# The SSD state product as three fp32r passes in a one-core hybrid decoder step

## The chip, the cores and the metric

One core of one Trainium2 chip runs the whole program. The metric is device time in microseconds (us) of one execution; the kernel before has a median of 1965.07 us over three runs (1964.24 to 1966.66). Less is better.

## What is computed

One inference step of a decoder layer: a norm, one combined input projection, three parallel groups (a gated linear recurrence, dilated-window attention, a Mamba-2 state-space group called SSD), and one output projection. The prompt has 2048 tokens, and 8 samples bring 4 tokens each. The change touches the SSD group of the prompt, which works through 16 chunks of 128 tokens and carries a state from chunk to chunk:

```python
xdt = x * dt[..., None]
scores = jnp.einsum('bcihn,bcjhn->bcijh', Ch, Bh) * decay
y_diag = jnp.einsum('bcijh,bcjhp->bcihp', scores, xdt)
to_end = jnp.exp(cum[:, :, -1:, :] - cum)
chunk_states = jnp.einsum('bcjhn,bcjh,bcjhp->bchpn', Bh, to_end, xdt)
...
h_last, h_starts = lax.scan(step, h0, ...)     # h = chunk_decay * h + chunk_states
y_off = jnp.einsum('bcihn,bchpn->bcihp', Ch, h_starts) * jnp.exp(cum)[..., None]
```

`chunk_states` is the product that the change rewrites: B transposed, times x·dt·to_end, for each chunk.

## The kernel before, in words

The program runs in stages: norm and input projections, the samples, attention, and from about 1440 us on the last stage, in which the output projection of chunk c and the SSD of the chunks ahead of it run interleaved.

Large products are made in three fp32r passes by `mm3` (lines 81 to 84): each operand is split into a high part in fp32r and a low part (the rest), and high·high, high·low and low·high are summed in PSUM. The output projection `out_chunk` (line 1434) does this for each chunk: 2 halves of the model width times 16 weight tiles times 3 passes of 128x512, 96 matmuls (tile `ops`). After each of the 32 steps it may let the SSD generator `ssd_part` (line 1270) take one step, 15 SSD steps to 32 projection steps. A framework schedules each engine's instructions in one fixed order and sets the waits; each engine runs its order without overtaking.

The SSD of a chunk has two head groups, g = 0 and 1. For each:

- `ssd_open` (line 694, once a chunk): `gp`, the products of C and B; `gm`, their mask, on DVE; `tpb`, B transposed on PE, copied by ACT to the one tile `bt` (line 710).
- `ssd_decay` (line 719): ACT takes exp(cum) from the freshly loaded `sg` into `ecB`; DVE subtracts in eight pieces (line 728), ACT takes the exponential (line 730), DVE multiplies by `gm` (line 731).
- `ssd_x` (line 734): PE transposes x (`tpx`), DVE multiplies by dt to `xdt` (line 744), POOL multiplies that by `tend` into the tile `xte` (line 750), and x by D (line 1292).
- `yd` (line 1298, from `sg` and `xdt`) and `yo` (line 1303, from the state `hT`) on PE.
- DVE forms y in four steps (lines 1311 to 1314): `yo` times `ecB`, plus `yd`, plus `xb`, times the gate `zt`. `yd` and `yo` are in PSUM, all else in SBUF.
- `group_norm` (line 754): ACT squares, POOL adds twice (lines 758, 759), PE sums over partitions (`rs`), ACT makes the reciprocal norm `rB`, DVE multiplies (line 766).
- the state product `stp` (line 1322), one fp32 matmul of 128x512 that PE carries out as two instructions; POOL decays `hT` (line 1327) and DVE adds `stp` (line 1328).
- the split of y for the output projection: ACT `sh` (line 1335), DVE `sl` (line 1336).

Chunk 0 runs on slab tiles (`ssd_early`, line 1248) while attention ends, and only it forms `xte` late (line 1320). The tile `sg` has one buffer: the load for the next half is issued when `yd` has read the last one. Weight tiles of the output projection (`wo`) are still being loaded and split on ACT and DVE (lines 1009, 1010) while chunks 0 and 1 run.

```python
xte = ck.tile([128, 8, 64], F32, tag="xte", name="xte", bufs=1)
pool.tensor_tensor(out=xte[:n], in0=xdt[:n], in1=tend[...], op=OP.mult)
...
pe.matmul(stp, lhsT=bt[:, g], rhs=xte.rearrange("p h d -> p (h d)"), start=True, stop=True)
```

Of the kernel before, what the change touches and what calls it, by code (L numbers as in the profile page):

```python
# [32 lines left out]
def tile_hybrid_step(ctx: ExitStack, tc: tile.TileContext, A):  # L33
# [1214 lines left out]
    def ssd_early():  # L1248
# [9 lines left out]
        ck0.own = {"gm": [piece(c_[0], 512, 2)], "bt": [piece(c_[0], 768, 2)], "xdt": [piece(c_[2], 512, 8, 64), piece(c_[3], 0, 8, 64)]}  # L1258
        for g in range(2):
# [10 lines left out]
    def ssd_part(c):  # L1270
# [5 lines left out]
        for g in range(2 if c == 0 else 0):  # L1276
            sg = ssd_decay(c, g, ck, gm)
            yield
            xb, xdt, _ = ssd_x(c, g, ck, ps6, False)
            pool.tensor_tensor(out=xb, in0=xb, in1=dF[:, 4 * g:4 * g + 4, None].to_broadcast([128, 4, 128]), op=OP.mult)  # L1280
            ahead[g] = sg, xb, xdt
            yield
        for g in range(2):
# [38 lines left out]
            pe.matmul(stp, lhsT=bt[:, g], rhs=xte.rearrange("p h d -> p (h d)"), start=True, stop=True)  # L1322
            if c == 0:
# [326 lines left out]
```

## Time and profile before

| what | value |
|---|---|
| median of 3 runs | 1965.07 us (1964.24 to 1966.66) |
| the profiled execution | 1966.87 us, of which its span is 1965.1 us |
| PE busy | 1906.4 us, 97% of the span |
| DVE, ACT, POOL busy | 1065.2 us (54%), 780.9 us (40%), 271.9 us (14%) |
| granted TensorE clock over the span | 0.992 of full speed |
| state product `stp` | 32 products, 64 matmul instructions |

The span is the time between the first and last recorded instruction; the rest of the 1966.87 us lies around it. A busy PE is not a PE at its peak: matmuls overlap, so a duration of one is longer than the distance from its start to the next start, and that distance is what a pass costs. Names stand as output<-inputs; buffer numbers are left out. The number in brackets behind a timeline row is the idle time of that engine just before it, and what ended it.

### The profile page before, as it was taken

To read this page: it belongs to the slowest core of one execution; us is meant where nothing else is said; L and a number is where in the kernel's file an instruction comes from. 1 tells how busy PE (TensorE), PEld (TensorE's weight loads), DVE (VectorE), ACT (ScalarE), POOL (GpSimd) and SP (SyncE) were. 2 spreads that over 40 slices of the span, in tenths; PEclk is the share of its full clock that TensorE was granted. 3 is DMA by queue.
4 is the path that set the end of the run, shared out by engine and by line. 5 is a ranking of instruction groups with operands and counts; after the bars stand their busy time and mean duration, and the time that the engine had idled before them with its cause. 6 is when DMAs were issued, how large, how long until landed. Compare 5 with 4: busy or idle time off the path is not lost.

```text
span 1965.1 us, 35826 instructions
## 1 busy us (share of the span) xinstructions
PE 1906.4 (97%) x14178; PEld 1559.9 (79%) x14178; DVE 1065.2 (54%) x2338; ACT 780.9 (40%) x1530; POOL 271.9 (14%) x346
## 2 busy tenths in 40 slices
PE   7999999999999999999999899999998999999998
PEld 7998888888888888887866686777776878677876
DVE  7414444444423666664322215666777777667774
ACT  6412637272712222223133315666564333324332
POOL 0100111111110111111000100000012232322231
PEclk9999999999999999998999999999999999999999
DMA  7422121121223222225477651442375444434441
GB/s 234 127 83 67 46 65 54 55 76 55 76 83 95 72 78 67 72 68 148 139 199 201 185 185 52 145 137 77 116 216 156 140 128 128 124 110 131 124 140 65
DMA packets 278388, 222.03 MB, mean 113 GB/s; under 512 B 34738, under 2 KB 234402, under 8 KB 278220
## 3 DMA queue, kind: packets, MB, share of 16 engines
q1 hardware_dynamic: 278220, 219.73, 37.3%
q8 instruction: 112, 1.84, 0.4%
q14 instruction: 56, 0.46, 0.1%
HBM read 150.81 MB, written 68.86 MB: 112 GB/s over the span
## 4 chain that ended last, share of the span: by engine, by line
PE 85%; DMA 4%; ACT 4%; DVE 3%; issue 1%; SPq 1%; POOL 1%; DVEq 0%; ACTq 0%; POOLq 0%
PE mm L82 15%; PE mm L84 15%; PE mm L83 15%; PE ops L84 5%; PE ops L83 5%; PE ops L82 5%; PE pt L1179 3%; ACT sr L1151 2%; PE o L1215 2%; PE s L1124 2%; PE yd L1298 2%; PE yo L1303 1%; PE s L1103 1%; DMA x<-in_x_prompt_dram 1%; PE mmt L82 1%
## 5 line engine op out<-in xcount | busy, mean ns | idle before, releaser
L82 PE MATMUL mm<-xh,wh 128*128 128x512 f32 (+2 forms) x1600 | 563.3, 352 | 1.6 <-DVE h L846 0.9
L83 PE MATMUL mm<-xl,wh 128*128 128x512 f32 (+2 forms) x1600 | 561.7, 351 | 0.0
L84 PE MATMUL mm<-xh,wl 128*128 128x512 f32 (+2 forms) x1600 | 561.0, 351 | 0.0
L82 PEld LDWEIGHTS mm<-xh,wh 128*128 128x128 f32 x1600 | 301.7, 189 | 44.0 <-issue 4.3
L84 PEld LDWEIGHTS mm<-xh,wl 128*128 128x128 f32 x1600 | 300.9, 188 | 41.0 <-issue 2.9
L83 PEld LDWEIGHTS mm<-xl,wh 128*128 128x128 f32 x1600 | 301.4, 188 | 39.0 <-issue 1.7
L146 POOL TENSOR_TENSOR wr<-wr,gC 128x1024 f32<-128x1024 f32 x40 | 79.1, 1978 | 415.7 <-DMA wr<-in_w_in_dram 370.8
L443 DVE SCALAR_TENSOR_TENSOR o<-u,ssdc,o 128x512 f32<-128x512 f32 (+1 forms) x216 | 128.8, 617 | 5.1
L1151 ACT ACTIVATE sr<-sr,nm 128x384 f32<-128x384 f32 (+3 forms) x128 | 97.9, 771 | 23.3 <-DVE nm L1147 14.1
L650 ACT ACTIVATE o<-o 128x512 f32<-128x512 f32 (+2 forms) x60 | 33.1, 552 | 149.4 <-DVE o L443 77.3
L148 DVE SCALAR_TENSOR_TENSOR wl<-wr,wh 128x1024 fp32r<-128x1024 f32 x40 | 48.9, 1223 | 68.4 <-ACT wh L147 68.4
L1062 ACT COPY ptsb<-pt 128x512 f32<-128x512 f32 x96 | 52.5, 583 | 75.0 <-PE pt L1179 74.9
L728 DVE TENSOR_SCALAR sg<-sg,cum 128x128 f32<-128x128 f32 (+1 forms) x256 | 72.9, 344 | 16.5 <-ACT ecB L726 16.5
L82 PE MATMUL mmt<-wh,xh 128*128 128x256 f32 (+3 forms) x272 | 78.5, 291 | 1.6 <-ACT xh L254 0.8
L83 PE MATMUL mmt<-wl,xh 128*128 128x256 f32 (+3 forms) x272 | 77.8, 287 | 0.3
L1179 PE MATMUL pt<-ident,sr 128*128 128x128 f32 x576 | 75.2, 281 | 2.8 <-ACT sr L1151 1.8
L84 PE MATMUL mmt<-wh,xl 128*128 128x256 f32 (+3 forms) x272 | 77.9, 288 | 0.0
L1112 DVE CUSTOM_DVE_ANT_1 sr<-s,bias 128x256 f32<-128x256 f32 x128 | 46.5, 419 | 56.9 <-PE s L1124 29.7
L441 DVE TENSOR_SCALAR o<-u,ssdc 128x512 f32<-128x512 f32 (+1 forms) x72 | 40.5, 575 | 65.8 <-ACT u L423 57.6
L1179 PEld LDWEIGHTS pt<-ident,sr 128*128 128x128 f32 x576 | 63.6, 143 | 15.1 <-issue 8.8
L423 ACT COPY u<-mm 128x512 f32<-128x512 f32 (+1 forms) x80 | 39.6, 495 | 88.6 <-PE mm L84 79.6
L726 ACT ACTIVATE ecB<-sg 64x512 f32<-64x512 f32 x60 | 37.8, 630 | 91.7 <-DMA sg<-d_cum 77.1
(526 smaller groups left out, 3585.0 us busy)
## 6 DMA issues: line engine op xcount, KB each, us to landing
wr<-in_w_in_dram SPq DMA_DIRECT2D x40, 512.0 KB
sg<-d_cum SPq DMA_DIRECT2D x30, 512.0 KB
d_xbc<-o SPq DMA_DIRECT2D x36, 256.0 KB
x<-in_x_prompt_dram SPq DMA_DIRECT2D x32, 256.0 KB
kc<-in_cache_attn_k_dram SPq DMA_DIRECT2D x32, 256.0 KB
vt<-in_cache_attn_v_dram SPq DMA_DIRECT2D x32, 256.0 KB
xres<-in_x_prompt_dram SPq DMA_DIRECT2D x32, 256.0 KB
out_dram<-ot SPq DMA_DIRECT2D x32, 256.0 KB
```

Source lines behind the costliest of these rows:

```text
L82: pe.matmul(out, lhsT=wh, rhs=xh, start=start, stop=False)
L83: pe.matmul(out, lhsT=wh, rhs=xl, start=False, stop=False)
L84: pe.matmul(out, lhsT=wl, rhs=xh, start=False, stop=stop)
L146: pool.tensor_tensor(out=wr, in0=wr, in1=gC[:, :, None].to_broadcast([128, 8, 128]), op=OP.mult)
L148: dve.scalar_tensor_tensor(out=wl, in0=wr, scalar=scale, in1=wh.bitcast(F32), op0=OP.mult, op1=OP.subtract)
L441: dve.tensor_scalar(out=o, in0=v(0), scalar1=w[:, 0:1], scalar2=b, op0=OP.mult, op1=OP.add)
L443: dve.scalar_tensor_tensor(out=o, in0=v(t), scalar=w[:, t:t + 1], in1=o, op0=OP.mult, op1=OP.add)
L728: dve.tensor_scalar(out=sg[:n, h], in0=sg[:n, h], scalar1=cum[:n, c, 8 * g + h:8 * g + h + 1], scalar2=0.0, op0=OP.subtract, op1=OP.min)
L1062: act.copy(out=out, in_=in_)
L1112: dve.tensor_tensor_reduce(out=sr[e][r][:, nk:].rearrange("p (w c) -> p w c", w=2), in0=pw[e][:, j].rearrange("p (w c) -> p w c", w=2), in ...
L1151: act.activation(out=sr[e][r], in_=sr[e][r], func=AF.Exp, bias=nm[:, e, r:r + 1], accum_out=ll[:, e, r:r + 1])
L1179: pe.transpose(tp[:, r], sr[e][r][:, 128 * g:128 * g + 128], ident)
```

## The change

The state product becomes three fp32r passes through `mm3`. For that, `bt` becomes a pair of tiles (ACT casts the high part, DVE subtracts for the low part), and `xte` becomes a pair: POOL multiplies `xdt` by `tend` in place, ACT casts it to the high part, POOL subtracts for the low part. Since `xdt` is overwritten, the product with `tend` moves from `ssd_x` to behind the forming of y, for every chunk, and `xdt` gets two buffers. `ecB` goes: exp(cum) is written into the tile `y`, which is allocated earlier. `rB` gets one buffer, and four small constant tiles move to a pool that closes before the last stage. Lines of the kernel after stand up to four higher than before.

```diff
-        bt = ck.tile([128, 2, 128], F32, tag="bt", name="bt", bufs=1)
+        bt = [ck.tile([128, 2, 128], F32R, tag=f"bt{i}", name="bt", bufs=1) for i in "hl"]
...
-        act.copy(out=bt, in_=tp[:, 0:2])
+        act.copy(out=bt[0], in_=tp[:, 0:2])
+        dve.tensor_tensor(out=bt[1], in0=tp[:, 0:2], in1=bt[0].bitcast(F32), op=OP.subtract)
...
-        xdt = ck.tile([128, 8, 64], F32, tag="xdt", name="xdt", bufs=1)
+        xdt = ck.tile([128, 8, 64], F32, tag="xdt", name="xdt", bufs=2)
...
     def to_end(c, g, ck, xdt):
-        n = TT[c][1]
-        xte = ck.tile([128, 8, 64], F32, tag="xte", name="xte", bufs=1)
-        pool.tensor_tensor(out=xte[:n], in0=xdt[:n], in1=tend[:n, c, 8 * g:8 * g + 8, None].to_broadcast([n, 8, 64]),
-                           op=OP.mult)
-        return xte
+        xh_, xl_ = [ck.tile([128, 512], F32R, tag=f"xte{i}", name="xte", bufs=1) for i in "hl"]
+        xte = xdt.rearrange("p h d -> p (h d)")
+        pool.tensor_tensor(out=xdt, in0=xdt, in1=tend[:, c, 8 * g:8 * g + 8, None].to_broadcast([128, 8, 64]), op=OP.mult)
+        act.copy(out=xh_, in_=xte)
+        pool.tensor_tensor(out=xl_, in0=xte, in1=xh_.bitcast(F32), op=OP.subtract)
+        return xh_, xl_
...
-                ecB = ck.tile([128, 4, 128], F32, tag="ecB", name="ecB", bufs=1)
-                sg = ssd_decay(c, g, ck, gm, ecB)
+                y = ck.tile([128, 4, 128], F32, tag="yt", name="y")
+                sg = ssd_decay(c, g, ck, gm, y)
                 yield
-                xb, xdt, xte = ssd_x(c, g, ck, ps6)
+                xb, xdt = ssd_x(c, g, ck, ps6)
...
-                dve.tensor_tensor(out=y, in0=yo, in1=ecB, op=OP.mult)
+                dve.tensor_tensor(out=y, in0=y, in1=yo, op=OP.mult)
...
             yield
+            xte = to_end(c, g, ck, xdt)
             norm = group_norm(ck, ps6, y, 128, dve if c == 0 else pool)
             next(norm)
             yield
-            if c == 0:
-                xte = to_end(c, g, ck, xdt)
             stp = psA.tile([128, 512], F32, tag="mm", name="stp")
-            pe.matmul(stp, lhsT=bt[:, g], rhs=xte.rearrange("p h d -> p (h d)"), start=True, stop=True)
+            mm3(stp, bt[0][:, g], bt[1][:, g], *xte, True, True)
```

How the orders of two engines change, at a place that repeats from chunk 3 to chunk 15. On POOL, one half of a chunk, before: the product with D, the product with `tend`, the decay of the state, the two sums of squares.

```order
L1292 TENSOR_TENSOR xb<-xb,dF 128x512
L750 TENSOR_TENSOR xte<-xdt,tend 128x512
L1327 TENSOR_TENSOR hT<-hT,dec 128x512
L758 TENSOR_TENSOR sq<-sq 128x256
L759 TENSOR_TENSOR sq<-sq 128x128
```

The same half after the change:

```order
L1297 TENSOR_TENSOR xb<-xb,dF 128x512
L752 TENSOR_TENSOR xdt<-xdt,tend 128x512
L1331 TENSOR_TENSOR hT<-hT,dec 128x512
L754 TENSOR_TENSOR xte<-xdt,xte 128x512
L761 TENSOR_TENSOR sq<-sq 128x256
L762 TENSOR_TENSOR sq<-sq 128x128
```

The product with `tend` is now the in-place one, in the same place of the order; the low part of `xte` stands behind the decay of the state, and ahead of the sums.

On ACT, from the reciprocal norm of a chunk's second half to the split of the next chunk's rows, before:

```order
L764 ACTIVATE rB<-rs,eps_t 128x128
L765 ACTIVATE rB<-rB 128x128
L1335 CAST sh<-y 128x512
L710 COPY bt<-tpb 128x256
L730 ACTIVATE sg<-sg 128x1024
L1443 CAST mh<-ym 128x512
```

and after:

```order
L767 ACTIVATE rB<-rs,eps_t 128x128
L768 ACTIVATE rB<-rB 128x128
L710 CAST bt<-tpb 128x256
L1339 CAST sh<-y 128x512
L731 ACTIVATE sg<-sg 128x1024
L753 CAST xte<-xdt 128x512
L1447 CAST mh<-ym 128x512
```

The transposed B is now cast ahead of `sh` and not behind it, and the high part of `xte` stands behind the exponential. On DVE one row comes in per chunk, the low part of `bt`, between `gm` and the last piece of the subtraction. On PE the two instructions of `stp` become three, in the same places from chunk 3 on; in chunks 0 to 2 the order of PE, DVE and ACT is mixed anew.

## Rows read from the trace of the kernel before

**Rows 1.** The page: busy time per engine; shares of the chain that ended last.
```profile
PE 1906.4 (97%) x14178; PEld 1559.9 (79%) x14178; DVE 1065.2 (54%) x2338; ACT 780.9 (40%) x1530; POOL 271.9 (14%) x346
...
PE 85%; DMA 4%; ACT 4%; DVE 3%; issue 1%; SPq 1%; POOL 1%; DVEq 0%; ACTq 0%; POOLq 0%
```

**Rows 2.** Busy time by stretch: us, PE, PEld, DVE, ACT, POOL busy (x), clock, DMA, GB/s.
```profile
1440.00:1500.00 60.00, 54.07 (x333) 38.86 (x331) 52.31 (x87) 33.23 (x57) 16.72 (x15) 1.00 0.66 193
1500.00:1940.00 440.00, 435.73 (x2444) 339.20 (x2445) 307.44 (x592) 160.11 (x334) 128.12 (x144) 1.00 0.41 124
```

**Rows 3.** PE timeline around one state product: start, us, engine, line, operation, [idle].
```profile
1633.53 0.39 PE L83 MATMUL ops<-wo11l,sh 128*128 128x512 f32 x1
1633.76 0.39 PE L84 MATMUL ops<-wo11h,sl 128*128 128x512 f32 x1
1633.98 1.02 PE L1322 MATMUL stp<-xte,bt 128*128 128x512 f32 x2
1635.08 0.40 PE L83 MATMUL ops<-wo12l,sh 128*128 128x512 f32 x1
```

**Rows 4.** The chain that ended last, around the same product: start, us, what.
```profile
1634.14 0.86 PE stp L1322 x2
```

**Rows 5.** DVE timeline of the second half of a chunk.
```profile
1629.38 0.69 DVE L1311 TENSOR_TENSOR y<-yo,ecB 128x512 f32<-128x512 f32 x1 [2.61 <-PE yo L1303]
1630.10 0.69 DVE L1312 TENSOR_TENSOR y<-y,yd 128x512 f32<-128x512 f32 x1
1630.89 0.69 DVE L1313 TENSOR_TENSOR y<-y,xb 128x512 f32<-128x512 f32 x1
1631.62 0.69 DVE L1314 TENSOR_TENSOR y<-y,zt 128x512 f32<-128x512 f32 x1
1640.08 0.68 DVE L744 TENSOR_TENSOR xdt<-tpx,dtT 128x512 f32<-128x512 f32 x1
```

**Rows 6.** PEld timeline: first weight load of yd in four halves.
```profile
1536.17 0.85 PEld L1298 LDWEIGHTS yd<-sg,xdt 128*64 128x64 f32 x16 [0.36 <-DVE xdt L744]
...
1641.11 0.85 PEld L1298 LDWEIGHTS yd<-sg,xdt 128*64 128x64 f32 x16 [0.35 <-DVE xdt L744]
...
1765.14 0.85 PEld L1298 LDWEIGHTS yd<-sg,xdt 128*64 128x64 f32 x16 [0.43 <-DVE xdt L744]
...
1915.19 0.85 PEld L1298 LDWEIGHTS yd<-sg,xdt 128*64 128x64 f32 x16 [0.36 <-DVE xdt L744]
```

**Rows 7.** POOL timeline of the same half as rows 5.
```profile
1627.03 1.04 POOL L750 TENSOR_TENSOR xte<-xdt,tend 128x512 f32<-128x512 f32 x1
1629.42 1.05 POOL L1327 TENSOR_TENSOR hT<-hT,dec 128x512 f32<-128x512 f32 x1 [1.35 <-PE yo L1303]
```

**Rows 8.** DVE, then POOL, at the first chunk: operations of both at once.
```profile
1452.74 1.03 DVE L1314 TENSOR_TENSOR y<-y,c 128x512 f32<-128x512 f32 x1
...
1452.17 1.05 POOL L750 TENSOR_TENSOR xte<-c,tend 128x512 f32<-128x512 f32 x1 [3.17 <-DVE wo7l L1010]
```

**Rows 9.** DVE timeline, end of a first half (to 1765), and two further xdt.
```profile
1535.24 0.68 DVE L744 TENSOR_TENSOR xdt<-tpx,dtT 128x512 f32<-128x512 f32 x1
...
1761.26 0.41 DVE L703 TENSOR_TENSOR gm<-gp,tri 128x256 f32<-128x256 f32 x1
1761.59 0.27 DVE L728 TENSOR_SCALAR sg<-sg,cum 128x128 f32<-128x128 f32 x1
1764.41 0.68 DVE L744 TENSOR_TENSOR xdt<-tpx,dtT 128x512 f32<-128x512 f32 x1
...
1914.33 0.68 DVE L744 TENSOR_TENSOR xdt<-tpx,dtT 128x512 f32<-128x512 f32 x1
```

**Rows 10.** ACT timeline of the same first half.
```profile
1761.38 0.62 ACT L1335 CAST sh<-y 128x512 fp32r<-128x512 f32 x1 [2.14 <-DVE y L766]
1761.90 0.37 ACT L710 COPY bt<-tpb 128x256 f32<-128x256 f32 x1
1762.16 1.06 ACT L730 ACTIVATE sg<-sg 128x1024 f32<-128x1024 f32 x1
```

More of the change, by code (lines that the diff above doesn't have):

```diff
@@ L64, in tile_hybrid_step @@
     aB = const.tile([128, 16], F32, name="aB")
-    srep = const.tile([128, 2, 16], F32, name="srep")
+    srep = mid.tile([128, 2, 16], F32, name="srep")
     dec = const.tile([128, 17, 16], F32, name="dec")
@@ L70, in tile_hybrid_step @@
     pool.memset(ones, 1.0)
-    decs = const.tile([128, 8, NB], F32, name="decs")
-    bsel = const.tile([96, NB], F32, name="bsel")
+    decs = mid.tile([128, 8, NB], F32, name="decs")
+    bsel = mid.tile([96, NB], F32, name="bsel")
     qs = mid.tile([128, 4, NS], F32, name="qs")
@@ L77, in tile_hybrid_step @@
     fold = const.tile([128, NS], F32, name="fold")
-    sp8 = const.tile([128, 2, 4], F32, name="sp8")
+    sp8 = mid.tile([128, 2, 4], F32, name="sp8")
     ngc = const.tile([128, 8], F32, name="ngc")
@@ L732, in ssd_decay, with ssd_x @@
         return sg
-    def ssd_x(c, g, ck, ps, ends=True):
+    def ssd_x(c, g, ck, ps):
         t0, n = TT[c]
@@ L742, in ssd_x @@
         xv = tp[:n].rearrange("p j (e d) -> p (j e) d", e=2)
-        xdt = ck.tile([128, 8, 64], F32, tag="xdt", name="xdt", bufs=1)
+        xdt = ck.tile([128, 8, 64], F32, tag="xdt", name="xdt", bufs=2)
         dve.tensor_tensor(out=xdt[:n], in0=xv, in1=dtT[:n, c, hs, None].to_broadcast([n, 8, 64]), op=OP.mult)
-        return xb, xdt, to_end(c, g, ck, xdt) if ends else None
+        return xb, xdt
     def to_end(c, g, ck, xdt):
-        n = TT[c][1]
-        xte = ck.tile([128, 8, 64], F32, tag="xte", name="xte", bufs=1)
-        pool.tensor_tensor(out=xte[:n], in0=xdt[:n], in1=tend[:n, c, 8 * g:8 * g + 8, None].to_broadcast([n, 8, 64]),
-                           op=OP.mult)
-        return xte
+        xh_, xl_ = [ck.tile([128, 512], F32R, tag=f"xte{i}", name="xte", bufs=1) for i in "hl"]
[4 more added lines that the diff above has]
+        return xh_, xl_
     def group_norm(ck, ps, y, n, add=pool):
@@ L762, in group_norm @@
         pe.matmul(rs[:, :n], lhsT=ones, rhs=sq[:, 0], start=True, stop=True)
-        rB = ck.tile([128, n], F32, tag="rB", name="rB")
+        rB = ck.tile([128, n], F32, tag="rB", name="rB", bufs=1)
         act.activation(out=rB, in_=rs[:, :n], func=AF.Ln, scale=1.0 / 512, bias=eps_t)
@@ L1251, in piece @@
             return t[:, o:o + m * n].rearrange("p (m t) -> p m t", m=m)
-        c_ = [big(f"c0{i}", XC, F32) for i in range(8)]
-        bc, tri0 = piece(c_[0], 0, 4), c_[7][:, 512:640]
+        c_ = [big(f"c0{i}", XC, F32R if i == 3 else F32) for i in range(8)]
+        bt = piece(c_[3], 512, 4)
+        bc, tri0 = piece(c_[0], 0, 4), c_[0][:, 768:896]
         sp.dma_start(out=bc, in_=d_xbc[1024:, 0:128].rearrange("(m p) t -> p m t", p=128))
@@ L1257, in ssd_early @@
         early[(0, "bc")], late["tri0"] = bc, tri0
-        ck0.own = {"gm": [piece(c_[0], 512, 2)], "bt": [piece(c_[0], 768, 2)], "xdt": [piece(c_[2], 512, 8, 64), piece(c_[3], 0, 8, 64)]}
+        ck0.own = {"gm": [piece(c_[0], 512, 2)], "bth": [bt[:, 0:2]], "btl": [bt[:, 2:4]], "xdt": [piece(c_[2], 512, 8, 64), piece(c_[7], 512, 8, 64)]}
         for g in range(2):
@@ L1278, in ssd_part @@
             yield
-            xb, xdt, _ = ssd_x(c, g, ck, ps6, False)
+            xb, xdt = ssd_x(c, g, ck, ps6)
             pool.tensor_tensor(out=xb, in0=xb, in1=dF[:, 4 * g:4 * g + 4, None].to_broadcast([128, 4, 128]), op=OP.mult)
@@ L1287, in ssd_part @@
             else:
-                ecB = ck.tile([128, 4, 128], F32, tag="ecB", name="ecB", bufs=1)
-                sg = ssd_decay(c, g, ck, gm, ecB)
+                y = ck.tile([128, 4, 128], F32, tag="yt", name="y")
+                sg = ssd_decay(c, g, ck, gm, y)
                 yield
-                xb, xdt, xte = ssd_x(c, g, ck, ps6)
+                xb, xdt = ssd_x(c, g, ck, ps6)
                 pool.tensor_tensor(out=xb, in0=xb, in1=dF[:, 4 * g:4 * g + 4, None].to_broadcast([128, 4, 128]), op=OP.mult)
@@ L1306, in ssd_part @@
             zt = load_z(ck, c, g)
-            y = ck.tile([128, 4, 128], F32, tag="yt", name="y")
             if c == 0:
+                y = ck.tile([128, 4, 128], F32, tag="yt", name="y")
                 dve.tensor_tensor(out=y, in0=yd, in1=xb, op=OP.add)
             else:
-                dve.tensor_tensor(out=y, in0=yo, in1=ecB, op=OP.mult)
+                dve.tensor_tensor(out=y, in0=y, in1=yo, op=OP.mult)
                 dve.tensor_tensor(out=y, in0=y, in1=yd, op=OP.add)
```

## The prediction

> **What bounds the kernel now.** I read the busy times and the chain first: PE is busy for 97% of the span, and 85% of the chain that ended last is PE [rows 1]. Then the stretches. From 1500 to 1940 us, where chunks 2 to 15 of the SSD run beside the output projection, PE is busy for 435.73 of 440 us; from 1440 to 1500, where chunks 0 and 1 run and weights are still being split, it is idle for 5.9 of 60 us, and DVE for 7.7 [rows 2]. So the last stage looks bound by PE, and a shorter state product should shorten it. Whether it does depends on how closely the other engines follow, and for that I read where `yd` starts.
>
> `yd` waits for `xdt` from DVE. In one half the first weight load came after 0.43 us of idle PEld, and it started 0.73 us after `xdt` had started (1764.41 to 1765.14); in the other rows it is 0.35 or 0.36 [rows 6, 9]. I read 0.35 as what the engine always shows there and 0.73 us as the path from the start of `xdt` to `yd`; what is left over 0.73 is slack. A chunk of about 30 us has two stretches:
>
> - A, from the first `yd` to the second, 13.95 us. At 1641.11 the slack is 1641.11 - 1640.08 - 0.73 = 0.30 us [rows 5, 6], and 0.19 to 0.33 in the other undisturbed ones.
> - B, from the second `yd` to the first of the next chunk, 16.03 us. Twelve such halves that nothing else disturbs have between 0 and 0.55 us of slack, 0.18 in the mean; the first of them 1536.17 - 1535.24 - 0.73 = 0.20, the last 1915.19 - 1914.33 - 0.73 = 0.13 [rows 6, 9].
>
> So PE sets the pace by a few tenths of a microsecond only, and the path through DVE, ACT and the load of `sg` is almost as long.
>
> **What PE gains.** A 128x512 fp32r pass costs the distance between starts, 1633.76 - 1633.53 = 0.23 us [rows 3]. The old product holds PE for 0.86 us [rows 4]; it also comes out of 1635.08 - 1633.98 - 0.23 = 0.87, since one projection pass lies between these starts [rows 3]. Three passes cost 0.69 us, so PE saves 0.17 us a product, and 32 of them save 5.4 us. The 0.39 us that a pass shows as its own duration is no price, as passes overlap; at that price three would cost 1.17 us. The FP8 and Floating Point Precision page of the Trainium skill (TensorE Precision Notes) counts true fp32 as four passes, so a product would lose one of four, a quarter of 0.86 or 0.215 us, 6.9 us in all (an estimate by that page); the rows' 0.23 for a pass leaves less.
>
> **The low part of `bt`**, 15 times on DVE and once for chunk 0, lies in stretch B between `gm` and the last piece of the subtraction. The nearest row is `gm`, which also reads 256 columns of PSUM: the next operation starts 0.33 us after it [rows 9]. ACT used to copy `bt` just ahead of the exponential, 1761.90 to 1762.16, while that last piece was done at about 1761.59 + 0.27 = 1761.86 [rows 9, 10]; in the new order the cast comes ahead of `sh`. So the exponential moves from 1762.16 to about 1761.86 + 0.33 + 0.06 = 1762.25, 0.09 later and not 0.33. Against a PE that is 0.17 us faster, `yd` then waits wherever the slack is under 0.26: with the twelve slacks 0.13 us in the mean. What is left of the gain is 0.04 us a half, and three of the twelve have an early load of `sg`, whose path the next paragraph lengthens. I count B as 0; its bounds are -0.17 and +0.33 - 0.18 = +0.15 us a half.
>
> **POOL.** Before, the product with `tend` ran ahead of `yd`'s end, 1627.03 to 1628.07, while DVE was idle [rows 7]. Now it waits until `yd` has read `xdt`, about 1628.3, and takes 1.04 us; the decay of `hT` follows at its old 1629.42 and ends at 1630.47 [rows 7]; then comes the new subtraction, 1.04 us, about 1630.45 to 1631.5. Its operands are there: the ACT cast, about as long as `sh` [rows 10], is done by 1630.1. The second pass of `stp` is due at 1633.98 + 0.23 = 1634.2 [rows 3], so PE has 2.7 us to spare there.
>
> But DVE works beside it. A DVE `y` times `zt` with both inputs in SBUF, 0.69 us alone, took 1.03 us from 1452.74 while POOL multiplied from 1452.17 to 1453.22; it ended 0.55 us after POOL did [rows 5, 8]. The first step of y, with one input in PSUM, kept its 0.69 us beside the decay of `hT` [rows 5, 7]. In the new order the subtraction runs when DVE comes to `y` plus `xb`, both in SBUF, at 1630.89 [rows 5]. It would end at about 1631.48 + 0.55 = 1632.03 and not at 1631.58: 0.45 us later. From there to `xdt` DVE's row of work is close to serial, so `xdt` moves by 0.45, past the slack of 0.30. Stretch A then takes 13.95 + 0.15 us, whatever PE saves. Fourteen such stretches, chunks 2 to 15: +2.1 us. The bounds for the hold are 0 (no contact: A gains 0.17 each, -2.4 us) and 0.85, if the subtraction starts just ahead of 1630.89 and holds DVE for its whole length.
>
> The SBUF — State Buffer page of the Trainium skill (Who interferes with whom) has the rule behind this: a VectorE instruction with two SBUF inputs and a GpSimd instruction that reads SBUF exclude each other, whichever issues first keeps the shared port pair for the whole instruction. The trace agrees in both rows; by the rule the hold could reach the whole subtraction, where the row showed 0.34 us.
>
> **Chunks 0 and 1** run between the weight splits. Their four products save 4 x 0.17 = 0.7 us on PE. Four subtractions come in on POOL, at 0 to 0.85 us of DVE each, 0.34 by the row [rows 8], and two low parts of `bt` at 0.33: 4 x 0.34 + 0.66 = 2.0 us for DVE, which has little to give [rows 2]. The scheduler also mixes the order anew. I charge the 2.0 in full and subtract 0.7: +1.3 us, between -0.7 and +3.4.
>
> The rest costs nothing: exp(cum) goes to another tile by the same instructions, 30 ACT casts, each about as long as `sh` [rows 10], fall where ACT waits (it is busy for 160 of 440 us [rows 2]), and the tiles that change pool or buffer count are free when their next writer comes.
>
> **Sum.** 2.1 + 0 + 1.3 = +3.4 us. On the profiled execution, 1966.87 (span 1965.1), that is 1970.3; on the median of the runs, 1.8 us lower, 1968.5 us.
>
> **The rivals.**
>
> PE alone sets the pace: the subtraction slips between DVE's operations, and the reordered ACT hides `bt`. Then the 5.4 us come through, 1959.7 us; without chunks 0 and 1 it is 4.7, 1960.4. For it speaks that PE is idle for so little [rows 2]; against it the slack of 0 to 0.3 us.
>
> The hold is longer, which ends slower: POOL's three operations back to back start a little later than I place them, and DVE's `y` plus `xb` waits longer. At a hold of 0.65 us, midway, A costs 14 x 0.35 = 4.9 and the sum is 6.2: 1971.3 us; at 0.85 it is 9.0 and 1974.1. It passes 0.2% (3.9 us) once the hold exceeds 0.49, that is 0.04 us more than I take. Against it: once the start falls behind 1630.89, DVE goes first.
>
> The subtraction comes too late for the second pass: only if it gives way to DVE until after 1633, 2.7 us later than placed. Each 0.1 us beyond costs 30 x 0.1 = 3 us. That the change does not do what it says is excluded by the order of PE: three passes stand at each product.
>
> **How the numbers follow.** A measurement of this kernel can tell about 0.2%, 3.9 us, from no change: the bounds are 1961.1 and 1969.0. The forecast, with part-gains between, has 0.42; PE alone 0.22; the longer hold 0.31 and the late pass 0.05. So faster 0.22, same 0.42, slower 0.36. The range reaches from the PE case to beyond the middle of the longer hold, 1960.0 to 1973.0. The likeliest single case alone spans 1966 to 1971.
>
> **What would show it.** In the profile after: three `stp` passes 0.23 us apart; stretch A at 14.1 and B at 16.0 us, with `yd` idle above 0.35 for `xdt`; `y` plus `xb` at about 1.1 us instead of 0.69, ending 0.55 us behind POOL's subtraction. If `y` plus `xb` keeps 0.69 us and A shrinks to 13.8, the hold is wrong; if `stp` waits for POOL, the late pass is right; if 1440 to 1500 carries the difference, I have mis-sized chunks 0 and 1.

## The result, and the profile after

The changed kernel takes 1978.65 us (median of four runs, 1977.51 to 1982.64) against 1965.87 us for the kernel before on the same chip: 1.0067 times the time, 95% interval 1.0052 to 1.0082. It is 12.8 us slower. The forecast was 1968.5 us with a range to 1973.0, so the sign of the likeliest case was right, the size was not, and the time lies outside the range.

The page of the profile after, beside [rows 1]: PE is still busy for 96% of the span, but its share of the chain that ended last fell from 85 to 70%, and DVE's rose from 3 to 13%.

```profile
PE 1903.5 (96%) x14210; PEld 1566.4 (79%) x14210; DVE 1091.7 (55%) x2354; ACT 802.3 (41%) x1562; POOL 313.8 (16%) x378
...
PE 70%; DVE 13%; ACT 8%; issue 3%; DMA 3%; POOL 1%; SPq 1%; DVEq 0%; ACTq 0%; POOLq 0%
```

The windows, beside [rows 2]: from 1500 to 1940 us PE is now idle for 20 of 440 us where it was idle for 4.

```profile
1440.00:1500.00 60.00, 53.70 (x331) 38.94 (x330) 52.09 (x79) 33.08 (x58) 20.74 (x17) 1.00 0.61 186
1500.00:1940.00 440.00, 420.26 (x2407) 333.92 (x2407) 325.30 (x604) 178.98 (x356) 163.71 (x169) 1.00 0.41 123
```

Where the time came in can be counted from three kinds of row: the first and the last pass of `ops`, and the first weight load of each `yd`. Before, the last stage ran 509.36 us from its first `ops` pass (1448.18) to its last (1957.54); after, 521.11 us. Up to the second `yd` of chunk 3 it lost 3.45 us (101.94 to 105.39), from there to the end 8.30 us (407.42 to 415.72). The stages ahead and the tail together differ by 1.1 us the other way, which makes the 10.6 us between the two profiled executions (1966.87 and 1977.51).

The PE timeline of the changed kernel shows the three passes 0.23 us apart, as expected:

```profile
1823.73 0.39 PE L82 MATMUL stp<-xte,bt 128*128 128x512 f32 x1
1823.96 0.39 PE L83 MATMUL stp<-xte,bt 128*128 128x512 f32 x1
1824.19 0.39 PE L84 MATMUL stp<-xte,bt 128*128 128x512 f32 x1
```

The PEld timeline, beside [rows 6]: 1644.89 to 1660.92 is a stretch B of 16.03 us, unchanged, and 1660.92 to 1675.67 a stretch A of 14.75 us, where it was 13.95. The twelve stretches A of chunks 4 to 15 are all 14.75 to 14.77 but one of 15.03, and their sum is 8.56 us above that of before. `yd` waits 1.36 us for `xdt`, of which 0.35 is what it always shows.

```profile
1644.89 0.85 PEld L1303 LDWEIGHTS yd<-sg,xdt 128*64 128x64 f32 x16 [1.36 <-DVE xdt L745]
...
1660.92 0.85 PEld L1303 LDWEIGHTS yd<-sg,xdt 128*64 128x64 f32 x16 [0.58 <-DVE xdt L745]
...
1675.67 0.85 PEld L1303 LDWEIGHTS yd<-sg,xdt 128*64 128x64 f32 x16 [1.36 <-DVE xdt L745]
```

The timeline of all engines over the same stretch A, beside [rows 5, 7], shows VectorE held twice:

```profile
1664.19 1.29 POOL L754 TENSOR_TENSOR xte<-xdt,xte 128x512 fp32r<-128x512 f32 x1
...
1664.66 1.37 DVE L1318 TENSOR_TENSOR y<-y,xb 128x512 f32<-128x512 f32 x1
...
1666.06 0.69 DVE L1319 TENSOR_TENSOR y<-y,zt 128x512 f32<-128x512 f32 x1
...
1673.43 1.04 POOL L1297 TENSOR_TENSOR xb<-xb,dF 128x512 f32<-128x512 f32 x1 [4.49 <-PE tpx L742]
...
1673.92 1.10 DVE L1340 TENSOR_TENSOR sl<-y,sh 128x512 fp32r<-128x512 f32 x1 [0.69 <-ACT sh L1339]
1674.94 0.68 DVE L745 TENSOR_TENSOR xdt<-tpx,dtT 128x512 f32<-128x512 f32 x1
```

First, POOL's subtraction (L754) begins 0.47 us ahead of `y` plus `xb` (L1318), which then takes 1.37 us and not 0.69; it ends at 1666.03, which is 0.55 us after POOL (1664.19 + 1.29 = 1665.48). That is the hold of the forecast, at 0.68 and not 0.45 us. Second, and not in the forecast at all: nine microseconds later the split of y (`sl`, L1340) meets POOL's product of `xb` with D (L1297), which began 0.49 us ahead of it. It takes 1.10 us and not 0.69, and again ends 0.55 us behind POOL (1674.47 and 1675.02). `xdt` and `yd` come directly behind it. The chain of waits now runs from one `yd` to the next through DVE and ACT, not through PE:

```profile
1664.66 1.38 DVE y L1318
...
1667.35 1.28 DVE sg L729 x5
...
1669.71 1.06 ACT sg L731
...
1673.27 0.63 ACT sh L1339
1673.92 1.10 DVE sl L1340
1675.02 0.61 DVE xdt L745
1675.67 1.09 PE yd L1303 x16
```

### The profile page after: what moved, and what is told of

It reads as the page before. It is cut to its first block, busy times and chain, and to the rows that moved or that the text cites. A ratio compares the mean times of both kernels' runs of the same rounds, so it can differ in the third digit from the quotient of the medians.

```text
span 1975.7 us, 35955 instructions
## 1 busy us (share of the span) xinstructions
PE 1903.5 (96%) x14210; PEld 1566.4 (79%) x14210; DVE 1091.7 (55%) x2354; ACT 802.3 (41%) x1562; POOL 313.8 (16%) x378
## 4 chain that ended last, share of the span: by engine, by line
PE 70%; DVE 13%; ACT 8%; issue 3%; DMA 3%; POOL 1%; SPq 1%; DVEq 0%; ACTq 0%; POOLq 0%
PE mm L82 15%; PE mm L84 15%; PE mm L83 15%; PE pt L1182 3%; ACT sr L1154 2%; PE o L1218 2%; PE s L1127 2%; DVE sg L729 2%; PE yd L1303 2%; DVE y L1318 1%; PE s L1106 1%; PE yo L1308 1%; PE mmt L82 1%; ACT sg L731 1%; PE mmt L83 1%
## 5 line engine op out<-in xcount | busy, mean ns | idle before, releaser
L82 PE MATMUL mm<-xh,wh 128*128 128x512 f32 (+2 forms) x1600 | 564.5, 353 | 1.7 <-ACT wh L147 0.9
L83 PE MATMUL mm<-xl,wh 128*128 128x512 f32 (+2 forms) x1600 | 563.0, 352 | 0.0
L82 PEld LDWEIGHTS mm<-xh,wh 128*128 128x128 f32 x1600 | 302.7, 189 | 44.2 <-issue 4.1
L83 PEld LDWEIGHTS mm<-xl,wh 128*128 128x128 f32 x1600 | 302.2, 189 | 38.8 <-issue 1.7
L443 DVE SCALAR_TENSOR_TENSOR o<-u,ssdc,o 128x512 f32<-128x512 f32 (+1 forms) x216 | 121.2, 582 | 5.1
L441 DVE TENSOR_SCALAR o<-u,ssdc 128x512 f32<-128x512 f32 (+1 forms) x72 | 46.8, 663 | 67.0 <-ACT u L423 58.9
L82 PE MATMUL mmt<-wh,xh 128*128 128x256 f32 (+3 forms) x272 | 79.3, 294 | 0.9 <-ACT xh L254 0.8
L83 PE MATMUL mmt<-wl,xh 128*128 128x256 f32 (+3 forms) x272 | 78.1, 288 | 0.0
L1182 PEld LDWEIGHTS pt<-ident,sr 128*128 128x128 f32 x576 | 63.5, 143 | 14.5 <-issue 8.7
L147 ACT ACTIVATE wh<-wr 128x1024 fp32r<-128x1024 f32 x40 | 42.4, 1061 | 74.3 <-PE mm L83 64.1
L1131 DVE CUSTOM_DVE_ANT_0 sr<-s,bias 128x128 f32<-128x128 f32 (+3 forms) x128 | 58.8, 487 | 24.1 <-PE s L1127 23.0
```

The source lines that it names most:

```text
L82: pe.matmul(out, lhsT=wh, rhs=xh, start=start, stop=False)
L83: pe.matmul(out, lhsT=wh, rhs=xl, start=False, stop=False)
L441: dve.tensor_scalar(out=o, in0=v(0), scalar1=w[:, 0:1], scalar2=b, op0=OP.mult, op1=OP.add)
L443: dve.scalar_tensor_tensor(out=o, in0=v(t), scalar=w[:, t:t + 1], in1=o, op0=OP.mult, op1=OP.add)
L1131: dve.tensor_tensor_reduce(out=sr[e][r][:, :nk], in0=ps[e][:, :nk], in1=bs[:, e, 512 - nk:512], scale=1.0, scalar=NEG, op0=OP.add, op1=OP. ...
L1182: pe.transpose(tp[:, r], sr[e][r][:, 128 * g:128 * g + 128], ident)
```

## The experiments

The stretches A and B of chunks 4 to 15 tell more than the times, since the order of the first chunks is mixed anew by nearly every edit. "First part" is from the first `ops` pass to the second `yd` of chunk 3, "second part" from there to the last `ops` pass, both in the profiled execution. A and B are the usual values of undisturbed stretches. (The expectations number the first chunks one too low: their "chunk 2" in this place is chunk 3.) The runs were made on several chips, so each ratio is against the kernel before on the same chip. A, B and the two parts come from one execution of each kernel, and in two cases from its longest: 1976.56 us in run 8, where the median is 1968.74, and 1969.17 us in run 11, where it is 1966.01.

| kernel | time, us | before there | ratio, 95% interval | A | B | first part | second part |
|---|---|---|---|---|---|---|---|
| before | 1965.87 | | | 13.96 | 16.03 | 101.94 | 407.42 |
| changed | 1978.65 | 1965.87 | 1.0067 (1.0052 to 1.0082) | 14.76 | 16.03 | 105.39 | 415.72 |
| changed, no low part of `xte` | 1968.68 | 1967.13 | 1.0001 (0.9981 to 1.0021) | 13.76, three 14.77 | 15.82 to 16.30 | 104.04 | 408.57 |
| changed, no product with D | 1971.16 | 1967.13 | 1.0024 (1.0007 to 1.0041) | 14.35 | 16.04 | 103.86 | 412.23 |
| before + subtraction ahead of the decay | 1966.35 | 1967.13 | 1.0008 (0.9990 to 1.0026) | 13.96 | 16.03 | 100.43 | 409.86 |
| before + three passes only | 1967.69 | 1967.13 | 1.0009 (0.9986 to 1.0031) | 13.77 | 15.81 | 108.72 | 402.20 |
| before + subtraction behind the decay | 1977.46 | 1965.39 | 1.0066 (1.0046 to 1.0085) | 14.97 | 16.13 | 101.75 | 421.10 |
| changed, low part of `bt` later | 1977.59 | 1965.39 | 1.0057 (1.0037 to 1.0077) | 14.77 | 15.82 | 105.32 | 416.62 |
| changed, early split of `xte` | 1974.97 | 1965.39 | 1.0046 (1.0030 to 1.0062) | 14.76 (8), 13.8 (4) | 15.82 to 16.09 | 107.28 | 412.17 |
| both of these | 1968.74 | 1965.39 | 1.0016 (1.0003 to 1.0029) | 14.77 (8), 13.77 (4) | 15.81 | 109.98 | 410.31 |
| both, and D on ScalarE | 1961.90 | 1967.38 | 0.9968 (0.9958 to 0.9978) | 13.8 | 15.82 | 105.29 | 403.47 |
| changed, D on ScalarE | 1971.74 | 1967.38 | 1.0021 (1.0010 to 1.0032) | 14.35 | 16.03 | 103.97 | 412.06 |
| before, D on ScalarE | 1966.01 | 1967.79 | 0.9992 (0.9980 to 1.0004) | 13.96 | 16.03 | 98.50 | 407.07 |

**1. The low part of `xte` left out.**

```diff
...
-        pool.tensor_tensor(out=xl_, in0=xte, in1=xh_.bitcast(F32), op=OP.subtract)
-        return xh_, xl_
+        return xh_, xh_
```

> The changed kernel with POOL's subtraction for the low part of xte left out (the third pass takes the high part again, so that product loses its low part). Chunks 0 to 2 are ordered anew by the scheduler, so the stretches of chunks 3 to 15 are the test. Theory (VectorE is held twice in stretch A, 0.68 us by this subtraction at y plus xb and about 0.4 us by the product with D at sl): y plus xb and sl both read 0.69 us, A falls from 14.76 to 13.78 us, which is the PE row of 13.95 less 0.17, B stays at 16.03; 12 to 13 stretches of 0.98 us less, so about 1966 us (1964 to 1969). Rival (the delay comes from the in-place product that waits for yd, from exp(cum) written into y, or from the three passes): A stays above 14.5 us and the time near 1978.

(It is the second pass, L83, that reads the low part of `xte`, not the third.) Eight of the twelve stretches A fell to 13.73 to 13.81 us, as the theory had it; that of chunk 8 reads 14.02. Three stayed at 14.77, though `y` plus `xb` took 0.69 us in every one: one hold can come without the other. In these three `sl` began 0.28 to 0.61 us later than in the fast ones (12.60 to 12.93 us behind `yd` and not 12.32), and behind the start of POOL's product.

**2. The product with D left out.**

```diff
-                pool.tensor_tensor(out=xb, in0=xb, in1=dF[:, 4 * g:4 * g + 4, None].to_broadcast([128, 4, 128]), op=OP.mult)
```

> The changed kernel with POOL's product of xb with D left out in chunks 1 to 15 (y gets x without the factor D). Every engine keeps its order, but for one reciprocal norm that changes its place. Theory: y plus xb still reads 1.37 us, as the subtraction holds it, but sl reads 0.69 in place of 1.0 to 1.1, so A falls by 0.33 to 0.41 to about 14.4 us, B stays at 16.03, and the time falls by some 12 x 0.35 = 4 us, to about 1974.5. Rival (the first hold alone makes the 0.8 us, and sl is longer but covered): A stays at 14.76 and the time at 1978.

A fell to 14.35 in eight stretches, as expected, 0.41 us below the changed kernel (14.48 to 14.79 in the other four). The time fell by more than the 4 us expected: it is 4.0 us above the kernel before on its chip, where the changed kernel is 12.8 above. The timeline of all engines in this run shows the first hold kept and the second gone:

```profile
1864.65 1.45 DVE L1317 TENSOR_TENSOR y<-y,xb 128x512 f32<-128x512 f32 x1
...
1874.00 0.69 DVE L1339 TENSOR_TENSOR sl<-y,sh 128x512 fp32r<-128x512 f32 x1 [0.69 <-ACT sh L1338]
...
1875.35 0.85 PEld L1302 LDWEIGHTS yd<-sg,xdt 128*64 128x64 f32 x16 [0.95 <-DVE xdt L745]
```

So the 0.80 us are made of the hold of `y` plus `xb` and of the hold of `sl`, not of one.

**3. The subtraction alone, added to the kernel before.**

```diff
+            if c:
+                pool.tensor_tensor(out=xdt, in0=xdt, in1=xte, op=OP.subtract)
             norm = group_norm(ck, ps6, y, 128, dve if c == 0 else pool)
```

> The kernel before with one POOL subtraction of 128x512 added in chunks 1 to 15, behind the decay of the state, its result never read (xdt minus xte into xdt, which is dead by then). Every other order is the one of before, and stp is the one fp32 matmul. Theory: the subtraction alone makes the loss. y plus xb reads 1.1 to 1.4 us, sl about 1.1, A goes from 13.95 to 14.5 to 14.75 us, B stays at 16.03, the time is 1973 to 1978 us. Rival (the loss is made by the other parts: bt, in-place product, three passes, pools): A under 14.2 and the time 1965 to 1968.

Here the expectation fell: A stayed at 13.96 in most stretches and the time did not move. The POOL and DVE rows of the run say why. The scheduler had put the added row ahead of the decay of the state, not behind it:

```profile
1760.63 1.04 POOL L750 TENSOR_TENSOR xte<-xdt,tend 128x512 f32<-128x512 f32 x1
...
1761.75 1.28 POOL L1317 TENSOR_TENSOR xdt<-xdt,xte 128x512 f32<-128x512 f32 x1
...
1762.99 1.05 POOL L1329 TENSOR_TENSOR hT<-hT,dec 128x512 f32<-128x512 f32 x1
...
1764.18 0.69 DVE L1313 TENSOR_TENSOR y<-y,xb 128x512 f32<-128x512 f32 x1
```

The subtraction (L1317) runs while DVE has nothing with two SBUF inputs to do, the decay ends at 1764.04, and `y` plus `xb` at 1764.18 is free. The edit did not test what it was meant to; it showed that 1.28 us more of POOL leave A as it was in that place.

**4. The three passes alone.**

```diff
...
-            pe.matmul(stp, lhsT=bt[:, g], rhs=xte.rearrange("p h d -> p (h d)"), start=True, stop=True)
+            xf = xte.rearrange("p h d -> p (h d)")
+            mm3(stp, bt[:, g], bt[:, g], xf, xf, True, True)
```

> The kernel before with the state product as three fp32r passes of high parts alone (bt cast by ACT, xte rounded by POOL's own product; both low parts left out, the passes repeat the high parts). This is the gain of PE by itself. Theory: A falls from 13.95 to 13.78 us, since DVE's path is 13.65; B falls from 16.03 to between 15.86 and 16.00, where the load of sg and DVE take over; the time is 1961 to 1964 us, give or take 2 us from chunks 0 to 2, which the scheduler orders anew. Rival (three passes cost as much as the fp32 matmul at this place): A 13.95, 1965 to 1967 us.

A 13.77 and B 15.81 us: PE's gain comes through in full, 0.19 and 0.22 us a product, and the second part is 5.2 us shorter than before. (One stretch A is 14.79: ACT waited 0.86 us for a late load of `sg` there, and `sl` began behind POOL's product.) The time still did not fall, 1967.69 us where 1961 to 1964 was expected, and the first part is 6.8 us longer in the profiled execution. The PEld timeline, beside [rows 6]:

```profile
1842.14 0.85 PEld L1298 LDWEIGHTS yd<-sg,xdt 128*64 128x64 f32 x16 [0.35 <-DVE xdt L744]
...
1857.95 0.85 PEld L1298 LDWEIGHTS yd<-sg,xdt 128*64 128x64 f32 x16 [0.36 <-issue]
...
1871.72 0.85 PEld L1298 LDWEIGHTS yd<-sg,xdt 128*64 128x64 f32 x16 [0.35 <-DVE xdt L744]
```

Those 6.8 us need not be the new order of the first chunks alone, since TensorE's granted clock (the third number from the end) was lower there. The windows of 20 us of the kernel before, then of this run:

```profile
1500.00:1520.00 20.00, 17.75 (x88) 13.89 (x89) 14.30 (x26) 7.08 (x14) 4.86 (x7) 0.91 0.43 133
...
1500.00:1520.00 20.00, 15.55 (x73) 11.77 (x71) 13.57 (x20) 5.29 (x11) 7.92 (x8) 0.83 0.44 132
```

Each is a mean between the clock's two levels, 2.4 and 1.2 GHz. In this run it also reads 0.91 from 1480 to 1500 and from 1520 to 1540, PE being busy for 17.20 and 18.96 us there, where the kernel before reads 1.00. That is 7.0 us of full clock lost against 1.8, so up to 5.2 of the 6.8 us (an estimate from these shares, as if PE had been busy throughout); how much the order costs stays open.

**5. The subtraction behind the decay.** The same row, made to read the decayed state so that it must stand behind it.

```diff
                 pool.tensor_tensor(out=hv, in0=hv, in1=dec[:, c, hs, None].to_broadcast([128, 8, 64]), op=OP.mult)
+                pool.tensor_tensor(out=xdt, in0=hv, in1=xte, op=OP.subtract)
```

> The kernel before with one POOL subtraction of 128x512 added in chunks 1 to 15, now certain to stand behind the decay of the state (it reads the decayed state and xte, and its result in xdt is never read). No other instruction changes place. Theory: the place of the subtraction makes the loss, not its existence. Behind the decay it begins 0.4 to 0.5 us ahead of y plus xb, so y plus xb reads about 1.37 us, sl about 1.1 where POOL's product with D meets it, A goes from 13.95 to 14.5 to 14.8 us, B stays at 16.0 to 16.1; 13 stretches of 0.6 to 0.85 us, 8 to 11 us above the kernel before on the same chip. Rival (the delay of the changed kernel comes from the in-place product, exp(cum) in y or the three passes): y plus xb 0.69, A 13.95, no change of the time, as in the run with the subtraction ahead of the decay.

This one row, whose result nobody reads, costs 12.1 us, as much as the whole change and more than the 8 to 11 expected. A is 14.97, above the 14.5 to 14.8 expected; the sum that gives this length stands in the next section. Every other instruction of the program stands where it stood. The timeline of all engines shows both holds:

```profile
1772.07 1.30 POOL L1328 TENSOR_TENSOR xdt<-hT,xte 128x512 f32<-128x512 f32 x1
...
1772.42 1.49 DVE L1313 TENSOR_TENSOR y<-y,xb 128x512 f32<-128x512 f32 x1
...
1781.41 1.04 POOL L1292 TENSOR_TENSOR xb<-xb,dF 128x512 f32<-128x512 f32 x1 [4.60 <-PE tpx L741]
...
1781.79 1.21 DVE L1337 TENSOR_TENSOR sl<-y,sh 128x512 fp32r<-128x512 f32 x1 [0.69 <-ACT sh L1336]
```

**6. The low part of `bt` later.**

```diff
-        dve.tensor_tensor(out=bt[1], in0=tp[:, 0:2], in1=bt[0].bitcast(F32), op=OP.subtract)
...
                 sg = ssd_decay(c, g, ck, gm, y)
+                if g == 0:
+                    dve.tensor_tensor(out=bt[1], in0=tpb[:, 0:2], in1=bt[0].bitcast(F32), op=OP.subtract)
```

> The changed kernel with the low part of bt moved on VectorE behind the last piece of the subtraction, so that ScalarE's exponential no longer waits for it. Orders differ from the changed kernel by this one row and by two or three rows beside it. Theory: 0.33 us of it stood in the path of stretch B; B falls from 16.03 to 15.8 to 15.9 us, A stays at 14.75, and the time falls by some 13 x 0.2 = 2.6 us against the changed kernel, to 1975 to 1977. Rival (the load of sg alone sets B): B stays at 16.03, 1978.

B fell to 15.82 as expected, so moving this subtraction gives PE's gain in B back. The time did not show it: beside eight short stretches, 1.7 us in all, this run has one of 16.54 and one of 19.34 us (16.02 and 17.74 in the changed kernel), which eat the gain. In both the load of `sg` was late: ACT began with it 6.09 to 6.20 us behind `yd`, and 4.85 to 5.37 behind it in the eight short ones.

**7. The split of `xte` early.** A tile of its own instead of the in-place product, so that POOL and ACT can split it while DVE is idle.

```diff
-        xdt = ck.tile([128, 8, 64], F32, tag="xdt", name="xdt", bufs=2)
+        xdt = ck.tile([128, 8, 64], F32, tag="xdt", name="xdt", bufs=1)
...
+                xte = to_end(c, g, ck, xdt, ck.tile([128, 8, 64], F32, tag="xtf", name="xtf", bufs=1))
...
-            xte = to_end(c, g, ck, xdt)
+            xte = to_end(c, g, ck, xdt) if c == 0 else xte
```

> The changed kernel with xte in a tile of its own again (xdt back to one buffer), so that for chunks 1 to 15 the product with tend, the cast and the subtraction run ahead of the decay of the state, while VectorE is idle; the three passes and bt stay. Theory: nothing of POOL meets y plus xb but the last 0.3 us of the decay, so y plus xb reads 0.7 to 0.95 us, sl 0.69, A falls from 14.76 to 13.8 us (at most 13.95), B stays at 16.03; 12 stretches of 0.9 us less than the changed kernel, 1966 to 1969 us. Rival (the three POOL operations back to back cost the same wherever they stand): A above 14.3, over 1973.

A miss, and the run that told the most. `y` plus `xb` fell to 0.69 to 1.09 us, as expected, but A took only two values, 13.8 in four stretches and 14.75 to 14.77 in seven (and 15.02 where the changed kernel has 15.03), whatever the first hold was. The timeline of all engines at the end of two stretches, a slow one and then a fast one:

```profile
1613.94 1.04 POOL L1298 TENSOR_TENSOR xb<-xb,dF 128x512 f32<-128x512 f32 x1 [4.95 <-PE tpx L742]
...
1613.96 1.57 DVE L1342 TENSOR_TENSOR sl<-y,sh 128x512 fp32r<-128x512 f32 x1 [0.69 <-ACT sh L1341]
...
1616.18 0.85 PEld L1305 LDWEIGHTS yd<-sg,xdt 128*64 128x64 f32 x16 [1.36 <-DVE xdt L745]
```

```profile
1783.65 0.69 DVE L1342 TENSOR_TENSOR sl<-y,sh 128x512 fp32r<-128x512 f32 x1 [0.69 <-ACT sh L1341]
...
1783.67 1.56 POOL L1298 TENSOR_TENSOR xb<-xb,dF 128x512 f32<-128x512 f32 x1 [5.01 <-PE tpx L742]
...
1784.99 0.85 PEld L1305 LDWEIGHTS yd<-sg,xdt 128*64 128x64 f32 x16 [0.43 <-DVE xdt L745]
```

In the first, POOL's product begins 0.02 us ahead of `sl`, `sl` takes 1.57 us and A is 14.75. In the second, `sl` begins 0.02 us ahead, it is POOL that takes 1.56, and A is 13.85. B, too, fell to 15.80 to 15.82 in five stretches, though `bt` stayed where it was. The place of POOL's product is set by PE (it waits for the transposes `tpx`), so the end of `sl` behind it, and with that A, is the same however little `sl` came late (14.75 to 14.77 for starts of `sl` from 12.53 to 13.32 us behind `yd`).

**8. Both edits together.**

> Both edits together: the early split of xte and the low part of bt behind the last piece of the subtraction. Theory: nothing but PE sets either stretch, A 13.8 and B 15.82 to 15.9 us as in the run with the passes alone; 14 stretches of 0.17 and 14 of 0.15 to 0.2 us below the kernel before, less the 2.4 us that chunks 0 to 2 lose in the changed kernel: 2 to 4 us below the kernel before. Rival (the gain of PE cannot be had beside this much work on VectorE): A or B at their old length, at or above the time before.

B is 15.81, A has the two values of run 7 again (four fast, eight slow), so the expectation failed at the same point. The time is 3.4 us above the kernel before. These stretches are of the longest of twelve executions; how many are slow in the others is not known.

**9. Both edits, and the product with D on ScalarE.**

```diff
-                pool.tensor_tensor(out=xb, in0=xb, in1=dF[:, 4 * g:4 * g + 4, None].to_broadcast([128, 4, 128]), op=OP.mult)
+                for m in range(4):
+                    act.activation(out=xb[:, m], in_=xb[:, m], func=AF.Copy, scale=dF[:, 4 * g + m:4 * g + m + 1])
```

> The early split of xte, the low part of bt behind the last piece, and, new, the product of xb with D on ScalarE (four activations of 128x128 with a scale for each partition) in place of POOL in chunks 1 to 15. Theory: stretch A has two values, and which it takes is settled by whether sl on VectorE or the product with D on POOL begins first; with nothing of POOL left at that point all stretches A read 13.77 us, none 14.75, and all undisturbed B 15.81; from the second yd of chunk 2 to the last pass of ops 402 to 404 us against 407.4 in the kernel before. Chunks 0 to 2 still lose 3 to 7 us, so the time is 1962 to 1967 us, between 3 us below and 2 us above the kernel before. Rival (DVE's path is too long in any case, or ScalarE now comes late with y plus xb): A above 14.0 in most chunks, over 1968.

With nothing of POOL beside `sl`, A is 13.76 to 13.87 us in nine stretches of twelve (14.00, 14.20 and 14.59 in the others; in the one of 14.59 `sg` had landed late), B 15.82, and the second part 403.47. The time is 5.5 us below the kernel before: 0.9968, 0.9958 to 0.9978. That is more than the 3 us expected at most; the second part gives 3.95 us of it, and where the rest comes from was not tried. This version beats both kernels. The same place in its timeline:

```profile
1774.51 1.28 ACT L1302 ACTIVATE xb<-xb,dF 128x128 f32<-128x128 f32 x4
...
1774.64 0.69 DVE L1346 TENSOR_TENSOR sl<-y,sh 128x512 fp32r<-128x512 f32 x1 [0.69 <-ACT sh L1345]
...
1775.98 0.85 PEld L1309 LDWEIGHTS yd<-sg,xdt 128*64 128x64 f32 x16 [0.43 <-DVE xdt L746]
```

**10. The same edit on the changed kernel alone.**

> The changed kernel with that one edit alone: the product of xb with D on ScalarE in chunks 1 to 15. Theory: y plus xb still reads 1.37 us, held by POOL's subtraction, but sl reads 0.69, so A falls from 14.76 to about 14.35 us, as in the run without the product; B stays at 16.03; some 12 x 0.42 = 5 us less than the changed kernel, 1972 to 1975 us. Rival (A is set by the first hold alone, or ScalarE's four activations come late): A at or above 14.7, 1977 or more.

A 14.35 us, as in run 2: the hold of `y` plus `xb` alone, 0.68 us less the slack. The time is 4.4 us above the kernel before.

**11. The same edit on the kernel before.**

> The kernel before with the product of xb with D on ScalarE in chunks 1 to 15, the one fp32 matmul kept. It shows whether the gain of the best version (early split, later bt, D on ScalarE) comes from the three passes or from the product that left POOL. Theory: the passes. Here PE still sets both stretches, A 13.95 and B 16.03 us, only the odd A of 14.97 goes; the time is that of the kernel before within 0.1%, give or take 2 us for the first chunks, whose order moves. Rival (POOL's product was in the way all along): A and B under 13.9 and 15.95, 1960 to 1963 us.

A and B as before in most stretches (the odd A is now one of 14.35), and no difference in the time that can be told. So the shorter A and B of run 9 are the gain of the three passes; taking POOL's product away only lets it through.

## Why the prediction was wrong, step by step

**The gain of PE** was right: 0.17 us a product forecast, 0.19 in A and 0.22 in B measured in run 4. The forecast's other estimate, 0.215, lies nearer to B. Why B gives 0.03 more was not tried.

**The low part of `bt`**: forecast to take the gain of B away, B 16.03. Measured 16.03, and 15.82 once it is moved (run 6): right in size, in part by luck. The reason is only a part of it: run 7 leaves `bt` where it was, takes most of the hold of `y` plus `xb` away and has 15.82 in five stretches. The hold falls in B as well (`y` plus `xb` takes 1.36 to 1.38 us there in the changed kernel), and the forecast let that count in three halves of twelve. It takes both: with the hold alone (run 6) or the low part of `bt` alone (runs 1 and 7) B is 15.82, unless the load of `sg` comes late. In run 1 ACT begins with `sg` 4.64 to 5.08 us behind `yd` in the three stretches of 15.82, and 5.34 to 5.55 behind it in the six of 16.08 to 16.30. The timeline of ACT in run 1, in a stretch of 15.82 (`yd` at 1748.38), then in the one of 16.30 (`yd` at 1838.47):

```profile
1753.43 0.63 ACT L727 ACTIVATE y<-sg 64x512 f32<-64x512 f32 x1 [2.16 <-DMA sg<-d_cum]
...
1844.03 0.63 ACT L727 ACTIVATE y<-sg 64x512 f32<-64x512 f32 x1 [2.66 <-DMA sg<-d_cum]
```

**POOL's subtraction**: its start was forecast 3.30 us behind `yd` and came 3.27 behind it (1664.19 - 1660.92). Its length was taken as 1.04 us, that of the products with a broadcast operand; it is 1.29. So the hold is 0.68 and not 0.45 us. The trace of the kernel before had nearer rows, POOL's sums of squares, whose two operands are both full:

```profile
1647.10 0.74 POOL L758 TENSOR_TENSOR sq<-sq 128x256 f32<-128x256 f32 x1 [2.67 <-ACT sq L757]
1647.91 0.46 POOL L759 TENSOR_TENSOR sq<-sq 128x128 f32<-128x128 f32 x1
```

128 columns more cost 0.28 us there, so 512 columns would take 0.46 + 3 x 0.28 = 1.30 us (an estimate from these two rows). By itself this mis-sized term makes A 13.65 + 0.68 = 14.33 us, and runs 2 and 10 show 14.35: +0.39 us a stretch where +0.15 was forecast. The other 0.41 of the 0.80 us is the next step.

**The step that failed** is the next one: "From there to `xdt` DVE's row of work is close to serial, so `xdt` moves by 0.45". It treats what stands between as a row that is shifted whole. But POOL's product with D stands beside the end of that row, and it is not shifted: it follows PE's `tpx`, and since PE is faster it even begins 0.22 us earlier after `yd` (1608.87 - 1596.14 = 12.73 us in the kernel before, and the same in run 5; 1673.43 - 1660.92 = 12.51 in the changed one). In the kernel before `sl` usually begins at 12.32, ahead by 0.41 us; with PE's gain the lead is 0.2 (12.51 - 12.32). Any delay above that lets POOL begin first. Then `sl` ends 0.55 us behind POOL, `xdt` begins 0.08 us ahead of that end, and `yd` 0.73 after it: 12.51 + 1.04 + 0.55 - 0.08 + 0.73 = 14.75 us, whatever the delay was, as long as `sl` begins while POOL's product still holds it back. Past a threshold the answer jumps by 1.0 us; it isn't the sum of the terms.

The trace of before had this very case, and I set it aside. One stretch A there is 14.97 us long (1596.14 to 1611.11) with 1.37 us of idle PEld, and I left it out of the slacks as disturbed. The timeline of all engines of the kernel before at that place:

```profile
1606.32 0.62 ACT L1443 CAST mh<-ym 128x512 fp32r<-128x512 f32 x1 [1.01 <-DMA ym<-d_y]
...
1608.87 1.04 POOL L1292 TENSOR_TENSOR xb<-xb,dF 128x512 f32<-128x512 f32 x1 [5.39 <-PE tpx L741]
1608.96 1.50 DVE L1336 TENSOR_TENSOR sl<-y,sh 128x512 fp32r<-128x512 f32 x1 [0.69 <-ACT sh L1335]
...
1610.38 0.68 DVE L744 TENSOR_TENSOR xdt<-tpx,dtT 128x512 f32<-128x512 f32 x1
...
1611.11 0.85 PEld L1298 LDWEIGHTS yd<-sg,xdt 128*64 128x64 f32 x16 [1.37 <-DVE xdt L744]
```

The load of `ym` is late, ACT waits 1.01 us for it, `sl` begins 0.50 us later than usual (1608.96 is 12.82 behind `yd`), POOL's product has begun 0.09 us earlier, and 0.5 us of delay turns into a stretch 1.0 us too long: 12.73 + 1.04 + 0.55 - 0.08 + 0.73 = 14.97. The price of the change stood in these rows.

**Chunks 0 and 1** were charged +1.3 us, and the stretches of chunks 2 and 3 +0.15 each, 1.6 in all; the first part grew by 3.45. The charge was to VectorE. Among the waits of PE in that part of the changed kernel are two that the kernel before has not:

```profile
PE stp L83 <- POOL xte L754: 3.5, 4, 1.3
...
PE stp L82 <- ACT xte L753: 1.1, 3, 0.6
```

In chunks 1 and 2 `stp` follows `yd` by 2.9 to 5.0 us and not by 6.83, and in four products from chunk 0 to chunk 2 the subtraction does come too late: the rival of the late second pass (L83), given 0.05 and priced at the steady state alone, holds here, with 3.5 us of waiting. The 1.1 us are the first pass (L82), which waits for ACT's cast. The wait is not the net loss: in run 1 it is gone, but PE waits 5.1 us for the sums of squares where it waited 3.6, and the first part is 104.04 us, only 1.35 less. The granted clock differs too: from 1500 to 1520 us it reads 0.91 in the kernel before and 1.00 in the changed one. How much of the 3.45 us is the late pass, the new order or the clock stays open; over all kernels here the first part lies between 98.50 and 109.98.

**The rivals.** PE alone setting the pace was wrong for this kernel and right for run 9. The longer hold was the nearest: it had the place and the sign, 1971.3 to 1974.1 us, but knew one contact where there are two. The Trainium skill's rule (SBUF — State Buffer, Who interferes with whom) that whichever of the two engines issues first keeps the shared ports for its whole instruction agrees with the trace in both directions: run 7 shows it with 0.02 us between them. (The pair takes 1.58 to 1.59 us there, where 0.69 and 1.04 one after the other would be 1.73.) I applied that rule to one pair of instructions and not to the others on the path.

## What to carry to other kernels

When an engine is delayed by a few tenths of a microsecond, walk down the whole row of work behind the delay and ask at each instruction who runs beside it and which of the two now begins first; an instruction paced by another engine does not move along. Where the order of two instructions decides, the cost is a step, not a slope, so the lead in the trace (here 0.41 us) is the number to compare with the delay. And read the odd stretch that one is tempted to leave out: it may be the experiment that one is about to pay for.

## What the runs showed of the hardware that was not expected

A POOL subtraction of two full 128x512 tiles takes 1.27 to 1.30 us, with an f32 result (runs 3 and 5) as with an fp32r one (the changed kernel), where a product with a broadcast operand takes 1.04 us at the same size. Whether the second full operand or the operation makes the difference was not tried. And the exclusion works both ways at a resolution of 0.02 us: the same pair, `sl` and POOL's product, costs DVE 0.9 us when POOL begins 0.02 us ahead (1.57 us), and costs POOL 0.5 us when DVE does (1.56 us).
